# A down projection in seven block products for eight, with two of the weights' block sums made by accumulating transfers

## The chip, the cores and the metric

The kernel runs on one core of a Trainium2 chip. The metric is the device time of one execution in microseconds. A core has a matrix engine (TensorE, PE in the profile; its weight loads are the row PEld), a vector engine (VectorE, DVE), an activation engine (ScalarE, ACT), a general engine (GpSimd, POOL) and SyncE (SP), which here issues the DMA transfers. Each engine works through its own queue in order, and the engines wait for one another on semaphores.

## The reference

Two layers of a bidirectional encoder on one sequence of 512 positions with 1024 channels, all in float32. The first half of a layer (a Fourier group beside windowed attention, then an output projection) is not touched by the change. The second half is this:

```python
h = rmsnorm(x, norm2[l])                                   # 512 x 1024
up = dwconv_centred(h @ w_up[l], conv_w[l], conv_b[l])     # 512 x 5632, three taps along the positions
gate, val = up[..., :D_FF], up[..., D_FF:]                 # D_FF = 2816
x = x + (jax.nn.silu(gate) * val) @ w_down[l]              # w_down is 2816 x 1024
```

## The kernel before, in words

Activations lie transposed: 128 channels on the partitions, 512 positions along the free axis. So `x` is 8 tiles `x[m]` of 128x512, and the hidden width of 2816 is 22 tiles of 128.

Every large product is made in three passes. An operand is split into a rounded high half and the remainder, its low half: ScalarE writes the high half, VectorE subtracts it for the low one (`split` for activations, `wsplit` for weights, lines 90 and 93). `mm3` (lines 120 to 122) then multiplies high by high, low by high and high by low into one PSUM accumulation. The split weights live in the tags `whi` and `wlo`, with 5 slots of 512 columns each; raw weights come into `wraw`, 3 slots of 1024 columns, loaded on SP.

The feed-forward part runs over `HALVES`, two runs of 11 hidden tiles. For each hidden tile `fi` the gate tile and the value tile (`z` = 0 and 1) are made: 8 input tiles x 3 matmuls of 512 columns, then VectorE multiplies by the norm's scale (`u`, out of PSUM), ScalarE applies the middle tap and the bias, and VectorE adds the two outer taps (two `stt`, line 96). SiLU on ScalarE, one product of gate and value (on VectorE in layer 0, on POOL in layer 1) and a split into two halves give the tile `gu[k]`, stored in pieces of the tags `slab`, `pT` and `m4`. Temporary tiles of 512 columns come from the tag `tF`, with 6 slots.

After a run's 11 tiles come its 8 output tiles. For each `m`, the weights of 11 hidden tiles are loaded and split, 33 matmuls of 512 columns go into one PSUM bank, and VectorE adds the bank to `x[m]`. The banks are taken in turn from `FFN_BANKS`, six of them. At the end of layer 1 each `x[m]` is stored as soon as it is final, the last one in two halves of 256 positions. At the end of layer 0 each final `x[m]` is also scaled and split for the next layer (`norm_tile`).

In layer 0 a generator, `presplit`, prepares the weights of layer 1's first half in between: for each of 44 keys (16 `qkv`, 8 `u`, 4 `f`, 16 `o`) it loads the raw weights (two keys in one transfer, into `m4`), folds the `u` and `f` ones with two VectorE sums, splits the result into `tA` and stores both halves to DRAM, to be fetched in layer 1. `next(ahead)` does one key: before, once in three weight tiles of the up projection and twice for each output tile.

The program's order on each engine isn't the order of the source: a scheduler places the instructions at build time, along the dependencies and the free slots.

Of the kernel before, what the change touches and what calls it, by code (L numbers as in the profile page):

```python
# [16 lines left out]
P = 128  # L17
D = 1024
S = 512
# [15 lines left out]
HALVES = [(0, 11), (11, 11)]  # L35


def encoder_kernel(tc, t):
# [29 lines left out]
    def f(x):  # L68
# [5 lines left out]
             "tA": (512, 6), "tF": (512, 6), "sq": (512, 2)}  # L74
# [74 lines left out]
    def presplit(l):  # L149

        late = []

        def keep(key, src):
            n = src.shape[-1]
            two = [temp(n, "tA", F32R) for _ in range(2)]
            split(two[0], two[1], src)
            kept[key] = [dp.tile([P, n], F32, tag=f"{key}{s}", name=nm("kept")) for s in range(2)]
            store()
            late.append(lambda: [nc.sync.dma_start(o, f(z)) for o, z in zip(kept[key], two)])

        def store():
            while late:
                late.pop()()

        def cols(src, n, step):
            def load():
                raw = temp(1024, "m4")
                nc.sync.dma_start(raw[:, :n], src)
                return [raw[:, c:c + step] for c in range(0, n, step)]
            return load  # L170

        def prepare(kind, raw):
            if kind == "u":
                return fold_wu(raw)
            return fold_wf(raw) if kind == "f" else raw

        jobs = []
        for grp in (1, 0):
            for kk in range(KT // 2):
                jobs.append((cols(t["w_qkv"][l, grp, kk], 768, 384), [f"qkv{grp}{2 * kk + i}" for i in range(2)]))  # L180
        for kk in range(KT // 2):
            jobs.append((lambda kk=kk: load_wu(l, kk, temp(1024, "m4")), [f"u{2 * kk + i}" for i in range(2)]))
        for j in range(NF):
            jobs.append((lambda j=j: [load_wf(l, j, temp(1024, "m4"))], [f"f{j}"]))
        for half in range(2):
            for mp in range(KT // 2):
                jobs.append((cols(t["w_o"][l, half, :, mp * 1024:(mp + 1) * 1024], 1024, 512),
                             [f"o{half}{2 * mp + i}" for i in range(2)]))
        got = jobs[0][0]()
        for n, (_, keys) in enumerate(jobs):  # L190
            for i, key in enumerate(keys):
                keep(key, prepare(key[0], got[i]))
                if i == len(keys) - 1 and n + 1 < len(jobs):
                    got = jobs[n + 1][0]()
                yield
        store()
        while True:
            yield
# [179 lines left out]
    for l in range(L):  # L378
# [326 lines left out]
        for f0, nf in HALVES:  # L705
            gu = []
            for fi in range(f0, f0 + nf):
                ys_ = []
                n = fi - f0
                for z in range(2):  # L710
# [18 lines left out]
                if n < 4:  # L729
                    a = pair("slab")  # L730
                elif n < 8:
                    if n % 2 == 0:
                        two = temp(2048, "pT", F32R).rearrange("p (n s q) -> p n s q", n=2, s=2)
                    a = two[:, n % 2]
                else:
                    a = pair("m4")
                split(a[:, 0, :], a[:, 1, :], ys_[0])
                gu.append(a)
            nxt = []
            for m in range(KT):  # L740
                next(ahead)
                next(ahead)
                w = []
                for c in range(0, nf, 8):
                    n = min(8, nf - c)
                    w += wchunks(t["w_down"][l, m, :, (f0 + c) * P:(f0 + c + n) * P], n * P)
                end = l == L - 1 and f0 + nf == FT
                nh = 2 if end and m == KT - 1 else 1
                for h in range(nh):
                    q0, q1 = h * S // nh, (h + 1) * S // nh  # L750
                    nps[0] += 1
                    o = psum(FFN_BANKS[nps[0] % len(FFN_BANKS)])[:, q0:q1]
# [4 lines left out]
                    if end:  # L757
                        nc.sync.dma_start(t["out"][m, :, q0:q1], x[m][:, q0:q1])
                if l < L - 1 and f0 + nf == FT:
                    nxt.append(norm_tile(m, g1[:, l + 1, :], acc))  # L760
            xg = nxt
# [88 lines left out]
```

## Time and profile before

| | |
|---|---|
| runs shown, median (lowest to highest) | 1057.82 us (1056.07 to 1059.76) |
| the profiled execution | 1056.14 us, of which 1054.3 us are the span of the trace |
| PE busy | 1038.2 us (98%) |
| DVE busy | 726.8 us (69%) |
| ACT busy | 507.9 us (48%) |
| POOL busy | 90.8 us (9%) |
| granted clock of PE | 0.999 |
| transfers | 140.03 MB, nearly all issued by SP |

The busy time of an engine is the union of its instructions' durations. A matmul's shown duration is longer than the distance to the next one's start, since matmuls are pipelined; what a row of them costs is that distance. The same holds in a smaller measure for VectorE. Names such as `wlo<-wraw,whi` give the output and inputs of an instruction by the program's tags, `ps` is PSUM, and a name after `<-` in brackets is what ended the engine's idle time before that instruction.

### The profile page before, as it was taken

The numbers are of one execution on the slowest core, as the hardware profiler recorded it, in microseconds if no ns is written. First come the engines' busy times: TensorE is split into PE (matmuls) and PEld (weight loads), VectorE is DVE, ScalarE is ACT, GpSimd is POOL, SyncE is SP. The second block draws the span as 40 slices with busy tenths as digits, with TensorE's granted clock in tenths as the row PEclk, the third lists the DMA queues.
The fourth block names the chain that finished last, engine by engine and source line by source line (L and its number), as shares of the span: only waits on it lengthen the run. The fifth ranks groups of instructions, "written<-read, shape, count | busy, mean of one in ns | idle before, by whom it ended". The sixth has DMA issues, their size and how long they took to land.

```text
span 1054.3 us, 14425 instructions
## 1 busy us (share of the span) xinstructions
PE 1038.2 (98%) x5107; PEld 873.2 (83%) x5107; DVE 726.8 (69%) x1384; ACT 507.9 (48%) x939; POOL 90.8 (9%) x164
## 2 busy tenths in 40 slices
PE   8998999999999999999999999999999999999998
PEld 8986778888888888888899887888888888888887
DVE  8878768697767777777519775478877336878632
ACT  5339755455444445455423785246554224454421
POOL 0004410000000000000000152001101000101100
PEclk9999999999999999999999999999999999999999
DMA  7232152332269833239856313333332333332241
GB/s 273 83 115 87 58 193 81 100 100 96 78 226 353 324 100 101 89 114 322 280 181 221 113 62 99 122 100 94 101 101 74 96 115 100 98 101 82 82 150 48
DMA packets 60475, 140.03 MB, mean 133 GB/s; under 512 B 6642, under 2 KB 22258, under 8 KB 60404
## 3 DMA queue, kind: packets, MB, share of 16 engines
q1 hardware_dynamic: 60404, 139.12, 40.5%
q8 instruction: 40, 0.66, 0.3%
q14 instruction: 31, 0.25, 0.1%
HBM read 116.02 MB, written 23.07 MB: 132 GB/s over the span
## 4 chain that ended last, share of the span: by engine, by line
PE 93%; DVE 2%; DMA 2%; ACT 1%; issue 1%; POOL 0%; SPq 0%; ACTq 0%; DVEq 0%; POOLq 0%
PE ps L122 28%; PE ps L120 28%; PE ps L121 28%; PE ps L118 3%; PE ps L548 2%; PE ps L541 2%; PE ps L529 1%; DMA wraw<-in_w_qkv_dram 1%; PE ps L234 1%; PE ps L227 1%; ACT tA L90 0%; DMA x<-in_xT_dram 0%; DVE tA L533 0%; ACT act L90 0%; PE ps L500 0%
## 5 line engine op out<-in xcount | busy, mean ns | idle before, releaser
L90 ACT ACTIVATE whi<-wraw 128x512 fp32r<-128x512 f32 (+1 forms) x296 | 182.0, 616 | 290.8 <-PE ps L122 278.4
L120 PE MATMUL ps<-act,whi 128*128 128x512 f32 x768 | 298.9, 390 | 0.0
L121 PE MATMUL ps<-act,wlo 128*128 128x512 f32 x768 | 298.3, 389 | 0.0
L122 PE MATMUL ps<-act,whi 128*128 128x512 f32 x768 | 298.2, 389 | 0.0
L93 DVE TENSOR_TENSOR wlo<-wraw,whi 128x512 fp32r<-128x512 f32 (+1 forms) x304 | 219.7, 726 | 103.4 <-ACT whi L90 102.0
L122 PEld LDWEIGHTS ps<-act,whi 128*128 128x128 f32 x768 | 144.2, 188 | 30.1
L120 PEld LDWEIGHTS ps<-act,whi 128*128 128x128 f32 x768 | 144.2, 188 | 29.7
L121 PEld LDWEIGHTS ps<-act,wlo 128*128 128x128 f32 x768 | 144.2, 188 | 29.7
L96 DVE SCALAR_TENSOR_TENSOR tF<-tF,pb,tF 128x511 f32<-128x511 f32 x176 | 133.5, 763 | 11.1 <-ACT tF L90 8.7
L93 DVE TENSOR_TENSOR tF<-ps,rb 128x512 f32<-128x512 f32 x104 | 71.2, 689 | 77.9 <-PE ps L122 64.7
L120 PE MATMUL ps<-slab,whi 128*128 128x512 f32 (+2 forms) x212 | 82.2, 388 | 0.0
L122 PE MATMUL ps<-slab,whi 128*128 128x512 f32 (+2 forms) x212 | 79.9, 380 | 0.4 <-DVE slab L93 0.3
L121 PE MATMUL ps<-slab,wlo 128*128 128x512 f32 (+2 forms) x212 | 80.0, 378 | 0.0
L90 ACT ACTIVATE tF<-tF,pb 128x512 f32<-128x512 f32 x88 | 71.7, 816 | 11.3 <-DVE tF L93 4.6
L93 DVE TENSOR_TENSOR x<-x,ps 128x512 f32<-128x512 f32 (+1 forms) x49 | 32.9, 674 | 36.5 <-PE ps L122 36.3
L93 POOL TENSOR_TENSOR tF<-tF,tF 128x512 f32<-128x512 f32 x22 | 30.2, 1371 | 256.1 <-DVE tF L96 224.1
L120 PE MATMUL ps<-pT,whi 128*128 128x512 f32 (+1 forms) x132 | 50.5, 383 | 0.0
L121 PE MATMUL ps<-pT,wlo 128*128 128x512 f32 (+1 forms) x132 | 50.5, 383 | 0.0
L122 PE MATMUL ps<-pT,whi 128*128 128x512 f32 (+1 forms) x132 | 50.5, 383 | 0.0
L538 POOL TENSOR_SCALAR tA<-tA,den 128x256 f32<-128x256 f32 (+1 forms) x64 | 37.4, 590 | 145.1 <-DVE den L537 144.6
L533 DVE CUSTOM_DVE_ANT_0 tA<-ps,pb,nsink 128x256 f32<-128x256 f32 (+1 forms) x64 | 37.8, 603 | 14.5 <-PE ps L529 9.7
L122 PEld LDWEIGHTS ps<-slab,whi 128*128 128x128 f32 x212 | 39.7, 188 | 8.3 <-DVE slab L93 0.9
(178 smaller groups left out, 1485.0 us busy)
## 6 DMA issues: line engine op xcount, KB each, us to landing
wraw<-in_w_up_dram SPq DMA_DIRECT2D x88, 512.0 KB, 3.5
wraw<-in_w_down_dram SPq DMA_DIRECT2D x32, 512.0 KB, 3.7
kept<-tA SPq DMA_DIRECT2D x56, 256.0 KB, 5.7
whi<-kept SPq DMA_DIRECT2D x28, 256.0 KB, 3.0
wlo<-kept SPq DMA_DIRECT2D x28, 256.0 KB, 3.0
kept<-tA SPq DMA_DIRECT2D x32, 192.0 KB, 4.4
wraw<-in_w_down_dram SPq DMA_DIRECT2D x32, 192.0 KB, 2.4
wraw<-in_w_o_dram SPq DMA_DIRECT2D x8, 512.0 KB, 3.7
```

The lines of the kernel that those rows point to most:

```text
L90: return nc.scalar.activation(out, in_, func, **kw)
L93: return (eng or nc.vector).tensor_tensor(out, a, b, op=op)
L96: return nc.vector.scalar_tensor_tensor(out=out, in0=a, scalar=s, in1=b, op0=op0, op1=op1)
L118: nc.tensor.matmul(out, a[0], b[0], start=start, stop=stop, **kw)
L120: nc.tensor.matmul(out, a[0], b[0], start=start, stop=False, **kw)
L121: nc.tensor.matmul(out, a[1], b[0], start=False, stop=False, **kw)
L122: nc.tensor.matmul(out, a[0], b[1], start=False, stop=stop, **kw)
L227: nc.tensor.matmul(pt[:, 2 * b:2 * b + 2], acc[:, b * P:(b + 1) * P], ones2, start=True, stop=True)
L533: nc.vector.tensor_tensor_reduce(out=pr[:, :n], in0=sc[:, :n], in1=mask[:, m0:m0 + n], scale=qs_scale[p][:, i, e:e + 1], scalar=nsink[:, l ...
L538: nc.gpsimd.tensor_scalar(pr[:, :n], pr[:, :n], den[:, i:i + 1], 1.0, op0=ALU.mult, op1=ALU.mult)
L541: tr = nc.tensor.transpose(pp[:, j * P:(j + 1) * P], pr[:, j * P:(j + 1) * P], ident)
L548: pv = nc.tensor.matmul(py[64 * e:64 * e + 64, i0 * P:(i1 + 1) * P], vp[:, j, 64 * g:64 * g + 64], pT[:, half, e, b0:b0 + 2 * (i1 - i0) + ...
```

## The change

The hidden tiles are now taken in three groups of 8, 8 and 6 (`GROUPS`), and in each group the down projection of two output tiles is treated as a product of 2x2 blocks. Of the weights, a block is one output tile by half of the group's hidden tiles (`kp` = 4, 4 or 3 of them): `a11, a12` belong to the even output tile, `a21, a22` to the odd one. Of the activations, a block is half of the group's hidden tiles by half of the positions (256 columns). Seven products of such blocks give the four output blocks, where the plain way takes eight.

Four sums of activation blocks are needed (`T1` to `T4`), made once a group by VectorE from each pair of hidden tiles (`seven_gu`), and then split: 7 halves of 256 columns for each pair, high and low, in the pieces that `pieces` hands out. For this the hidden tiles are made in the order 0, kp, 1, kp+1 and so on, so that a pair is complete after two tiles.

Four sums of weight blocks are needed for each pair of output tiles (a block row, four in a group; `seven_w`). `a21 + a22` is made by loading `a21` into `s1` on SP and then letting a transfer issued by POOL add `a22` onto it from DRAM. `s2 = a11 - s1` and `s3 = a11 - a21` are made by VectorE. When `s2` has been split for its own product, another transfer from POOL adds `a12` onto it. Each of the seven weight blocks is split by `wsplit`, which reads 512 or 384 columns.

The products go into three running sums, X, Y and Z. X and Y are the two halves of one PSUM tile, Z is half of another. After each product VectorE adds the sum as it then stands to a quarter of the two `x` tiles (128x256): X after products 0, 2, 4 and 6, Y after 1 and 5, Z after 3.

`presplit` now loads one key at a time, into a tag of its own (`praw`, 2 slots), and `next(ahead)` stands three times in four weight tiles of the up projection and once for each block row. The product of gate and value is on VectorE in both layers. The norm tiles at the end of layer 0 come two at a time, after a block row.

```diff
-HALVES = [(0, 11), (11, 11)]
+GROUPS = [(0, 8), (8, 8), (16, 6)]
...
-             "tA": (512, 6), "tF": (512, 6), "sq": (512, 2)}
+             "tA": (512, 6), "tF": (512, 6), "sq": (512, 2), "praw": (512, 2)}
...
+    LANDED = {3: (0, 0), 4: (1, 1), 5: (0, 1), 6: (1, 0)}
+    def pieces(kp):
+        for tag, n in (("slab", 2), ("pT", 5), ("m4", 2)):
+            for _ in range(TEMPS[tag][1]):
+                whole = temp(512 * n, tag, F32R)
+                yield from [whole[:, i * 512:(i + 1) * 512] for i in range(n)]
+
+    def seven_gu(b1, b2, room):
+        t13, t24 = temp(512, "tF"), temp(512, "tF")
+        lo, hi = slice(0, 256), slice(256, 512)
+        tt(t13[:, lo], b1[:, hi], b1[:, lo], ALU.subtract)
+        tt(t13[:, hi], b2[:, hi], b1[:, hi], ALU.subtract)
+        tt(t24[:, lo], t13[:, lo], b2[:, hi], ALU.subtract)
+        tt(t24[:, hi], t24[:, lo], b2[:, lo], ALU.add)
+        g = {}
+        one = next(room)
+        g["B11"] = [one[:, lo], one[:, hi]]
+        split(*g["B11"], b1[:, lo])
+        for src, keys in ((b2, ("B21", "B22")), (t13, ("T1", "T3")), (t24, ("T2", "T4"))):
+            two = [next(room), next(room)]
+            split(*two, src)
+            for key, cols in zip(keys, (lo, hi)):
+                g[key] = [z[:, cols] for z in two]
+        return g
+
+    def seven_w(l, m, f0, kp):
+        n = kp * P
+        a, b = [wload(t["w_down"][l, m + i, :, f0 * P:f0 * P + 2 * n], 2 * n) for i in range(2)]
+        s1 = temp(n, "tF")
+        nc.sync.dma_start(s1, t["w_down"][l, m + 1, :, f0 * P:f0 * P + n])
+        nc.gpsimd.dma_start(s1, t["w_down"][l, m + 1, :, f0 * P + n:f0 * P + 2 * n], accum_op=ALU.add)
+        a11, a12, a21, a22 = a[:, :n], a[:, n:], b[:, :n], b[:, n:]
+        yield "X", wsplit(a11), "B11", 0, 0
+        yield "Y", wsplit(s1), "T1", 1, 1
+        s2 = temp(n, "tF")
+        tt(s2, a11, s1, ALU.subtract)
+        yield "X", wsplit(s2), "T2", 0, 1
+        yield "Z", wsplit(a12), "B21", 0, 0
+        s3 = temp(n, "tF")
+        tt(s3, a11, a21, ALU.subtract)
+        yield "X", wsplit(s3), "T3", 1, 1
+        nc.gpsimd.dma_start(s2, t["w_down"][l, m, :, f0 * P + n:f0 * P + 2 * n], accum_op=ALU.add)
+        yield "Y", wsplit(s2), "B22", 0, 1
+        yield "X", wsplit(a22), "T4", 1, 0
...
-        for f0, nf in HALVES:
+        for f0, nf in GROUPS:
+            kp = nf // 2
+            room = pieces(kp)
             gu = []
-            for fi in range(f0, f0 + nf):
+            for n in range(nf):
+                fi = f0 + n // 2 + kp * (n % 2)
...
-                    if (2 * n + z) % 3 == 2:
+                    if (2 * n + z) % 4 < 3:
                         next(ahead)
                 act(ys_[0], ys_[0], AF.Silu)
-                tt(ys_[0], ys_[0], ys_[1], ALU.mult, nc.gpsimd if l else nc.vector)
...
+                tt(ys_[0], ys_[0], ys_[1], ALU.mult)
+                if n % 2 == 0:
+                    upper = ys_[0]
                 else:
-                    a = pair("m4")
-                split(a[:, 0, :], a[:, 1, :], ys_[0])
-                gu.append(a)
+                    gu.append(seven_gu(upper, ys_[0], room))
             nxt = []
-            for m in range(KT):
-                next(ahead)
+            for mp in range(KT // 2):
                 next(ahead)
...
-                    for k in range(nf):
-                        mm3(o, [z[:, (k % 4) * P:(k % 4 + 1) * P] for z in w[k // 4]],
-                            [gu[k][:, s, q0:q1] for s in range(2)], k == 0, k == nf - 1)
-                    tt(x[m][:, q0:q1], x[m][:, q0:q1], o, ALU.add)
...
+                xy, zz = [psum(FFN_BANKS[(nps[0] + i) % len(FFN_BANKS)]) for i in (1, 2)]
+                nps[0] += 2
+                bank = dict(X=xy[:, :256], Y=xy[:, 256:], Z=zz[:, :256])
+                for i, (b, w, g, r, c) in enumerate(seven_w(l, 2 * mp, f0, kp)):
+                    m, q0 = 2 * mp + r, 256 * c
+                    for k in range(kp):
+                        mm3(bank[b], [z[:, k * P:(k + 1) * P] for z in w], gu[k][g], k == 0 and i in (0, 3), k == kp - 1,
+                            skip_group_check=True)
+                    tt(x[m][:, q0:q0 + 256], x[m][:, q0:q0 + 256], bank[b], ALU.add)
+                    if l == L - 1 and f0 + nf == FT and i in LANDED:
+                        m, q0 = 2 * mp + LANDED[i][0], 256 * LANDED[i][1]
+                        nc.sync.dma_start(t["out"][m, :, q0:q0 + 256], x[m][:, q0:q0 + 256])
                 if l < L - 1 and f0 + nf == FT:
-                    nxt.append(norm_tile(m, g1[:, l + 1, :], acc))
+                    nxt += [norm_tile(m, g1[:, l + 1, :], acc) for m in (2 * mp, 2 * mp + 1)]
```

The rewritten `presplit` (one key a load) is left out of this cut.

More of the change, by code (lines that the diff above doesn't have):

```diff
@@ L163, in store, with load @@
                 late.pop()()
[L165 to L175, printed above, removed]
+        def load(src):
+            raw = temp(512, "praw")[:, :src.shape[-1]]
+            nc.sync.dma_start(raw, src)
+            return raw
@@ L177, in presplit @@
         jobs = []
         for grp in (1, 0):
[L179 to L182, printed above, removed]
+            for k in range(KT):
+                c = (k % 2) * 384
+                jobs.append((f"qkv{grp}{k}", lambda g=grp, k=k, c=c: load(t["w_qkv"][l, g, k // 2, :, c:c + 384])))
@@ L183, in presplit @@
+        for k in range(KT):
+            jobs.append((f"u{k}", lambda k=k: load(t["w_in"][l, k * P:(k + 1) * P, 0:FW])))
         for j in range(NF):
-            jobs.append((lambda j=j: [load_wf(l, j, temp(1024, "m4"))], [f"f{j}"]))
+            jobs.append((f"f{j}", lambda j=j: load_wf(l, j, temp(512, "praw"))))
         for half in range(2):
-            for mp in range(KT // 2):
-                jobs.append((cols(t["w_o"][l, half, :, mp * 1024:(mp + 1) * 1024], 1024, 512),
-                             [f"o{half}{2 * mp + i}" for i in range(2)]))
@@ L189, in presplit @@
[L189 to L195, printed above, removed]
+            for m in range(KT):
+                jobs.append((f"o{half}{m}", lambda h=half, m=m: load(t["w_o"][l, h, :, m * 512:(m + 1) * 512])))
+        got = jobs[0][1]()
+        for n, (key, _) in enumerate(jobs):
+            raw = got
+            if n + 1 < len(jobs):
+                got = jobs[n + 1][1]()
+            keep(key, fold_wu(raw) if key[0] == "u" else fold_wf(raw) if key[0] == "f" else raw)
+            yield
@@ L704, in encoder_kernel @@
         ahead = presplit(l + 1) if l < L - 1 else iter(lambda: 0, 1)
-        for f0, nf in HALVES:
+        for f0, nf in GROUPS:
+            kp = nf // 2
+            room = pieces(kp)
             gu = []
-            for fi in range(f0, f0 + nf):
+            for n in range(nf):
+                fi = f0 + n // 2 + kp * (n % 2)
                 ys_ = []
-                n = fi - f0
                 for z in range(2):
@@ L724, in encoder_kernel @@
                     ys_.append(y)
-                    if (2 * n + z) % 3 == 2:
+                    if (2 * n + z) % 4 < 3:
                         next(ahead)
                 act(ys_[0], ys_[0], AF.Silu)
-                tt(ys_[0], ys_[0], ys_[1], ALU.mult, nc.gpsimd if l else nc.vector)
[L729 to L734, printed above, removed]
-                else:
-                    a = pair("m4")
@@ L737, in encoder_kernel @@
-                split(a[:, 0, :], a[:, 1, :], ys_[0])
-                gu.append(a)
+                tt(ys_[0], ys_[0], ys_[1], ALU.mult)
+                if n % 2 == 0:
+                    upper = ys_[0]
+                else:
+                    gu.append(seven_gu(upper, ys_[0], room))
             nxt = []
-            for m in range(KT):
+            for mp in range(KT // 2):
                 next(ahead)
-                next(ahead)
[L743 to L752, printed above, removed]
-                    for k in range(nf):
-                        mm3(o, [z[:, (k % 4) * P:(k % 4 + 1) * P] for z in w[k // 4]],
-                            [gu[k][:, s, q0:q1] for s in range(2)], k == 0, k == nf - 1)
-                    tt(x[m][:, q0:q1], x[m][:, q0:q1], o, ALU.add)
-                    if end:
-                        nc.sync.dma_start(t["out"][m, :, q0:q1], x[m][:, q0:q1])
@@ L759, in encoder_kernel @@
                 if l < L - 1 and f0 + nf == FT:
-                    nxt.append(norm_tile(m, g1[:, l + 1, :], acc))
-            xg = nxt
+                    nxt += [norm_tile(m, g1[:, l + 1, :], acc) for m in (2 * mp, 2 * mp + 1)]
+        xg = nxt
     for cm in reversed(ctxs):
```

## The prediction

> **What bounds the kernel now.** I read the page's busy table and its chain first, then the windows of the feed-forward stages, then the timeline of single instructions.
>
> ```profile
> span 1054.3 us, 14425 instructions
> PE 1038.2 (98%) x5107; PEld 873.2 (83%) x5107; DVE 726.8 (69%) x1384; ACT 507.9 (48%) x939; POOL 90.8 (9%) x164
> PE 93%; DVE 2%; DMA 2%; ACT 1%; issue 1%; POOL 0%; SPq 0%; ACTq 0%; DVEq 0%; POOLq 0%
> ```
>
> The chain that ended last is 93% matmuls. In the windows (columns: stretch, length, busy time and count of PE, PEld, DVE, ACT, POOL, clock, DMA share, GB/s) PE is never idle in the feed-forward part of either layer:
>
> ```profile
> 195.00:295.00 100.00, 100.00 (x447) 82.92 (x446) 78.39 (x120) 53.31 (x81) 0.00 (x0) 1.00 0.30 94
> 300.00:358.00 58.00, 58.00 (x257) 48.03 (x256) 41.31 (x89) 25.22 (x46) 0.00 (x0) 1.00 0.98 348
> 720.00:815.00 95.00, 95.00 (x421) 78.67 (x420) 80.29 (x107) 51.22 (x76) 14.29 (x11) 1.00 0.29 92
> 820.00:875.00 55.00, 55.00 (x244) 45.56 (x243) 20.11 (x31) 13.92 (x23) 0.00 (x0) 1.00 0.33 104
> ...
> 200.00:210.00 10.00, 10.00 (x46) 8.26 (x45) 10.00 (x17) 8.22 (x12) 0.00 (x0) 1.00 0.29 85
> 210.00:220.00 10.00, 10.00 (x46) 8.29 (x45) 10.00 (x18) 5.74 (x9) 0.00 (x0) 1.00 0.30 87
> ```
>
> So PE time removed here is time gained, as long as nobody keeps PE waiting. The last two rows matter for that: VectorE was saturated for 20 us in a backlog and PE lost nothing.
>
> **Term 1, the matmuls.** Their price is the pitch from start to start, not the shown duration. The end of the down projection has both widths, because its last output tile is already cut into two halves of 256:
>
> ```profile
> 1035.73 0.39 PE L121 MATMUL ps<-slab,wlo 128*128 128x512 f32 x1
> ...
> 1042.76 0.39 PE L122 MATMUL ps<-m,whi 128*128 128x512 f32 x1
> 1042.98 0.28 PE L120 MATMUL ps<-slab,whi 128*128 128x256 f32 x1
> ...
> 1049.46 0.28 PE L120 MATMUL ps<-pT,whi 128*128 128x256 f32 x1
> ```
>
> 31 steps in 7.03 us are 0.2267 us for 512 columns; 54 steps in 6.48 us are 0.120 us for 256, each with a weight load of its own, so the doubled number of loads is in this price. Before: 8 tiles x 22 x 3 x 2 layers = 1056 matmuls of 512, 33 of them cut into 66 halves: 1023 x 0.2267 + 66 x 0.120 = 239.8 us. After: 7 products x 3 x (4+4+3 tile pairs) x 4 block rows x 2 layers = 1848 at 0.120, 221.8 us. Gain 18.1 us. All other terms are losses against it.
>
> **Term 2, VectorE.** Its price is a pitch too:
>
> ```profile
> 246.01 0.69 DVE L93 TENSOR_TENSOR tF<-ps,rb 128x512 f32<-128x512 f32 x1 [0.76 <-PE ps L122]
> 246.61 0.68 DVE L93 TENSOR_TENSOR pT<-tF,pT 128x512 fp32r<-128x512 f32 x1
> 247.22 0.68 DVE L93 TENSOR_TENSOR wlo<-wraw,whi 128x512 fp32r<-128x512 f32 x1
> 247.82 1.53 DVE L96 SCALAR_TENSOR_TENSOR tF<-tF,pb,tF 128x511 f32<-128x511 f32 x2
> 249.39 0.69 DVE L93 TENSOR_TENSOR wlo<-wraw,whi 128x512 fp32r<-128x512 f32 x1
> ...
> 312.34 0.55 DVE L93 TENSOR_TENSOR tA<-m,tA 128x384 fp32r<-128x384 f32 x1
> 312.81 0.69 DVE L93 TENSOR_TENSOR wlo<-wraw,whi 128x512 fp32r<-128x512 f32 x1
> ...
> 320.01 0.75 DVE L93 TENSOR_TENSOR tA<-m 128x255 f32<-128x255 f32 x2
> 320.68 0.69 DVE L93 TENSOR_TENSOR wlo<-wraw,whi 128x512 fp32r<-128x512 f32 x1
> ```
>
> 0.605 us for 512 columns, 0.47 for 384, 0.335 for 256, 1.57 for the pair of convolution steps. Up, per tile of the hidden width: 4 low halves of weights, 2 evacuations, 2 convolution pairs, 1 gating product, 4x0.605 + 1.2 + 3.14 + 0.6 = 7.4 us; before also one split (0.6), with the few prepared keys 8.3 of PE's 48 x 0.2267 = 10.88 (measured: 78.39 of 100). After, the split gives way per pair to four 256 sums, one 256 low half and three of 512, 5x0.335 + 3x0.605 = 3.5, or 1.75 a tile: 9.1 in layer 1. In layer 0, 33 instead of 14 prepared keys now fall into up (16 at 0.47, 8 folded `u` and 4 folded `f` at 2x0.335 + 0.605 and a small one, 1.4, 5 at 0.6: 27 us over 22 tiles), 10.4 of 10.88; the second group, with the folded keys, is over by about 0.4 x 8 tiles = 3 us.
>
> Down, per block row of four pairs: 7 low halves, 2 sums, 7 additions of 256, 9x0.605 + 7x0.335 = 7.8, plus 0.6 for a key in layer 0, against 84 x 0.120 = 10.08. With three pairs: 9x0.47 + 2.35 = 6.6 against 7.56. The last group of layer 0 also has two norm tiles (0.75 + 0.6 each, 2.7) and a key, 9.9: over by 2.4 x 4 = 9.6 us. Ends for the two overruns: 0 and 13. I take 2, near the lower end, because the saturated windows cost nothing and norms and keys can run on into the next projection, where VectorE has room.
>
> ScalarE: up 4x0.63 + 2x0.82 + 0.63 + 1.1 per tile, below 7 of 10.88 with the keys; down 4.4 to 7 of 7.56 or 10.08; nothing on the path.
>
> ```profile
> L90 ACT ACTIVATE whi<-wraw 128x512 fp32r<-128x512 f32 x256 | 161.2, 631 | 252.6 <-PE ps L122 247.7 <-DMA wraw<-in_w_down_dram 2.0 <-PE ps L118 1.3
> L90 ACT ACTIVATE tF<-tF,pb 128x512 f32<-128x512 f32 x88 | 71.7, 816 | 11.3 <-DVE tF L93 4.6 <-DVE tF L96 0.6
> ...
> L93 DVE TENSOR_TENSOR wlo<-wraw,whi 128x512 fp32r<-128x512 f32 x53 | 47.1, 889 | 17.5 <-ACT whi L90 17.1
> ...
> L93 DVE TENSOR_TENSOR wlo<-wraw,whi 128x512 fp32r<-128x512 f32 x108 | 74.4, 689 | 14.1 <-ACT whi L90 13.3
> ```
>
> The gating product of layer 1 goes from POOL to VectorE, 22 x 0.6 = 13 us more there. The last two rows are the weights' low halves in layer 1 after 878 us (889 ns) and in layer 0 (689 ns); the slow ones stand beside POOL's products (POOL 14.29 us busy in the 720 window), so about 0.2 us on each of some hundred comes back. Even; and POOL is free for the transfers.
>
> **Term 3, the hand-offs.** X and Y are halves of one PSUM tile, a running sum that is read after each product. If a read and a product in the same tile may not overlap, product 1 waits for the addition after product 0, 2 for 1, 4 for 2, 5 for 4 and 6 for 5. One hand-off from rows:
>
> ```profile
> 1046.82 0.28 PE L122 MATMUL ps<-m,whi 128*128 128x256 f32 x1
> 1047.14 0.42 DVE L93 TENSOR_TENSOR x<-x,ps 128x256 f32<-128x256 f32 x1 [3.27 <-PE ps L122]
> ...
> 117.32 1.89 DVE L93 TENSOR_TENSOR slab<-tF,slab 128x512 fp32r<-128x512 f32 x3
> 118.06 0.19 PEld L122 LDWEIGHTS ps<-slab,whi 128*128 128x128 f32 x1 [0.31 <-DVE slab L93]
> ```
>
> PE could go on at 1046.94; the addition ends at 1047.56; PE follows a VectorE result after 0.05 us (117.32 + 0.69 to 118.06): 0.67 us if nothing fills it. A filler is 9 or 12 matmuls, 1.08 or 1.44 us, so one is enough. Product 3, in Z, fills one of five; the others need the next block row, which has other banks (three pairs of six), but only five slots for split weights, so its first products are prepared late. Ends: 0, and 4 x 24 x 0.67 = 64 us. I take one open hand-off for two block rows, 12 x 0.67 = 8 us, near the lower end since PE's order before was interleaved where a tile was late.
>
> **Term 4, from up to down, six times.** The last activations need an evacuation, ACT's scaling, the convolution, the product, the two T1/T3 sums and a split: 0.6 + 0.82 + 1.57 + 0.6 + 0.67 + 0.63 + 0.69 = 5.6 us. PE has meanwhile product 0 whole (B11 comes from the earlier tile) and all but the last pair of 1 to 3: 12 + 27 matmuls, 4.7 us, or 9 + 18, 3.2 us; with the next row's product 0, 6.1 or 4.3. Between 2 x 1.3 and 2 x (0.9 + 0.9 + 2.4): I take 3.
>
> **Term 5, transfers.**
>
> ```profile
> wraw<-in_w_up_dram SPq DMA_DIRECT2D x88, 512.0 KB, 3.5
> kept<-tA SPq DMA_DIRECT2D x56, 256.0 KB, 5.7
> whi<-kept SPq DMA_DIRECT2D x28, 256.0 KB, 3.0
> m<-in_w_in_dram SPq DMA_DIRECT2D x4, 512.0 KB, 6.6
> ```
>
> SP issues three loads a block row for four, `w_down` moves seven blocks for four (104 GB/s of the 820 window to some 180), and of the keys' loads and stores only 12 of 44 stay in down: its share was 0.98 with PE full, so it eases; in up it rises from 0.30 to about 0.55 and the `w_up` loads queue behind keys on SP, three buffers ahead. Zero. POOL issues two accumulating transfers a row, none in the trace. The second starts when S2 is split and is used by product 5. Landing is bounded by 3.0 and 6.6 us, then 1.3 for a split; PE has products 2 to 4 in between (4.3 or 3.2 us) and up to four prepared ones ahead (another 5.8 or 4.3). With the lead: 0 for either. Without it: at 3.0, 8 x 1.1 = 9 us; at 6.6, 16 x 3.6 + 8 x 4.7 = 95 us. I take 0; POOL blocks nobody but its other transfer. [...]
>
> **Sum.** -18.1 + 2 + 8 + 3 + 0 = -5 us. The profiled execution took 1056.1 (span 1054.3 and 1.8 around it), 1.7 below the median of the three runs; from the two I forecast 1051 to 1053, and write 1052.
>
> **The rivals.**
> - *Everything hidden.* The hand-offs are all filled and VectorE's overruns vanish in the backlog: 1057.8 - 18 = 1040. For it: the saturated windows. Against: no stage had a chain of reads as tight as this.
> - *It comes out even.* One open hand-off per block row (16 us), 4 for overruns and transitions, +2: 1055 to 1061.
> - *The shared bank becomes the bound.* Place: products 1, 2, 4, 5, 6 of each block row. It decides from 1.1 open hand-offs a row on, with 2 a row 32 us, net +19, 1077; with 4, 1109. For it: five weight slots, and VectorE at 77 to 96%, where an addition queues behind a 0.6 us instruction. Against: three pairs of banks. [...]
> - *The accumulating transfer is late.* Half of the 95 us: 1057.8 - 5 + 48 = 1100. For it: nothing in the trace bounds it well. Against: plain loads of that size land in 3.0 us.
> - *Seven for eight isn't cheaper*, because a weight load of 188 ns must stand behind 256 columns: excluded by the 0.120 pitch.
>
> **How the numbers follow.** Forecast case (1045 to 1054) 0.30; all hidden 0.22; even 0.18; shared bank 0.19; late transfers 0.11. Less than 0.3%, 3.2 us, can't be told from no change here. Faster 0.52, same 0.18, slower 0.30. The range runs from 1039 (all hidden) to 1077 (two open hand-offs a row), which leaves out the worse halves of the last two. The likeliest case's own range is 1045 to 1054.
>
> **What would show it.** 1848 matmuls of 256 at a pitch of 0.120; PE under 100% only in the down windows, with gaps of 0.3 to 0.7 us released by the x additions (hand-offs), or by split weights behind a POOL transfer (late transfers); VectorE near 96% in layer 0's up. The forecast is wrong if PE in a down window is below 90% or at 100% throughout.

## The result, and the profile after

The changed kernel takes 1212.39 us (median of 4 runs, 1207.49 to 1217.4) against 1056.98 us on the same chip: 1.1467 times as long, 95% interval 1.1446 to 1.1488. The forecast was 1052 us, with 1077 as the upper end. The page of the changed kernel (busy times, then tenths in 40 slices, then the shares of the chain that ended last):

```profile
span 1205.6 us, 16704 instructions
PE 1062.4 (88%) x5866; PEld 919.9 (76%) x5866; DVE 876.3 (73%) x1793; ACT 557.4 (46%) x1055; POOL 105.3 (9%) x190
PE   8999989990899967999589999999969998699967
PEclk9999999995799988999899999999979999899979
PE 35%; DMA 7%; DVE 5%; issue 3%; ACT 1%; POOL 0%; SPq 0%; POOLq 0%; ACTq 0%; DVEq 0%
```

The span grew by 151.3 us. PE's idle time went from 16.1 (1054.3 - 1038.2) to 143.2 us (1205.6 - 1062.4): 127 of the 151. The other 24 are in PE's busy time, though the matmuls are 18 us less work. By the trace's clock records PE was busy for 55 us at half clock, which at a pitch of 0.213 for 0.120 us is 24 us of lost time; the remaining 18 are, by estimate, what 68 more interruptions leave as ends of a shown matmul beyond its pitch (0.28 - 0.12 to 0.58 - 0.21 us each, 11 to 25 us). The row of PE has a hole at each of six places, where a group's up projection (up) ends and its down projection (down) begins; these places are called seams below. The row of the clock is below 9 at or right after the same places.

How the two layers took it is read from two windows, each from the last attention product of a layer to the first of the next, or to the end (columns as in the prediction: stretch, length, PE, PEld, DVE, ACT, POOL, clock, DMA share, GB/s). Before:

```profile
145.00:610.30 465.30, 462.58 (x2241) 393.19 (x2237) 330.08 (x599) 225.78 (x384) 9.65 (x22) 1.00 0.51 168
661.40:1051.10 389.70, 389.66 (x1767) 324.05 (x1763) 246.74 (x344) 159.72 (x245) 32.18 (x24) 1.00 0.31 98
```

After:

```profile
145.30:701.60 556.30, 476.68 (x2635) 416.85 (x2631) 408.98 (x795) 251.15 (x445) 32.95 (x46) 0.94 0.54 159
752.50:1202.40 449.90, 399.84 (x2130) 347.37 (x2126) 318.68 (x558) 184.81 (x303) 22.83 (x26) 0.94 0.38 104
```

So 91 us were lost in layer 0, which has the next layer's presplit beside it, and 60 in layer 1, which has none. In the windows of up PE stays full; the loss sits at the seams. One of them, layer 1's first, in windows of 10 us and then in the timeline of all engines (matmuls left out between the last before and the first after the gap):

```profile
860.00:870.00 10.00, 10.00 (x48) 8.32 (x47) 6.21 (x11) 3.20 (x5) 0.00 (x0) 1.00 0.11 44
870.00:880.00 10.00, 1.19 (x10) 0.98 (x9) 6.34 (x12) 2.60 (x4) 1.81 (x2) 0.76 0.36 78
880.00:890.00 10.00, 7.71 (x36) 7.21 (x36) 5.96 (x11) 3.18 (x6) 0.86 (x1) 0.56 0.63 132
```

```profile
869.80 0.69 DVE L93 TENSOR_TENSOR tF<-ps,rb 128x512 f32<-128x512 f32 x1 [2.27 <-PE ps L122]
...
870.91 0.28 PE L122 MATMUL ps<-m,whi 128*128 128x256 f32 x1
...
873.13 1.49 DVE L93 TENSOR_TENSOR tF<-tF,tF 128x512 f32<-128x512 f32 x3
873.18 2.77 SPq L407 DMA_DIRECT2D tF<-in_w_down_dram  x2
...
876.33 0.94 POOL L408 DMA_DIRECT2D tF<-in_w_down_dram  x1 [75.49 <-ACT m L90]
...
880.75 0.69 DVE L93 TENSOR_TENSOR tF<-wraw,tF 128x512 f32<-128x512 f32 x1 [3.80 <-DMA tF<-in_w_down_dram]
880.81 1.36 ACT L90 ACTIVATE whi<-tF 128x512 fp32r<-128x512 f32 x2 [4.59 <-DMA tF<-in_w_down_dram]
881.36 0.69 DVE L93 TENSOR_TENSOR tF<-wraw,wraw 128x512 f32<-128x512 f32 x1
881.49 0.58 PE L120 MATMUL ps<-slab,whi 128*128 128x256 f32 x1 [10.30 <-DVE tF L93]
```

The sum `s1` is the weight of product 1, and its slot comes from `tF`, whose six slots hold up's evacuations and convolution results. SP can issue its load only at 873.18, when the last outer tap is done, after 14.4 us of waiting for the slot; POOL's accumulating transfer goes at 876.33 and its data are there at 880.75. PE had done product 0 by 871.19 and then stood for 10.30 us: 2.0 until the load was issued, 3.2 until the accumulating transfer was, 4.4 until its data were there, and 0.7 for the split. The kernel as a whole, in the waits and the transfers (KB, median us from issue to landing):

```profile
ACT whi L90 <- DMA tF<-in_w_down_dram: 96.7, 26, 7.2
POOL tF L408 <- DMA tF<-in_w_down_dram: 84.2, 18, 7.7
PE ps L120 <- DVE tF L93: 39.9, 5, 10.3
PE ps L120 <- ACT whi L90: 38.4, 14, 9.6
```

```profile
tF<-in_w_down_dram POOLq DMA_DIRECT2D x32, 256.0 KB, 4.3
tF<-in_w_down_dram SPq DMA_DIRECT2D x16, 256.0 KB, 5.3
```

The load's 5.3 us are a median over both layers; in the seam shown it landed after 2.6 us, and the rest of that gap is the wait for the slot and the accumulating transfer.

After the gap, the same matmuls go at half the pace for a while (PE alone in the timeline):

```profile
883.72 0.41 PE L122 MATMUL ps<-pT,whi 128*128 128x256 f32 x1
883.93 0.41 PE L120 MATMUL ps<-pT,whi 128*128 128x256 f32 x1
...
889.07 0.28 PE L121 MATMUL ps<-m,wlo 128*128 128x256 f32 x1
889.19 0.28 PE L122 MATMUL ps<-m,whi 128*128 128x256 f32 x1
```

The steps are 0.213 us up to 888.6 and 0.120 from then on, as the granted clock of 0.56 in the window from 880 to 890 says.

### The profile page after: what moved, and what is told of

The parts are those of the page before. It is cut to its first block, busy times and chain, and to the rows that moved or that the text cites. A ratio compares the mean times of both kernels' runs of the same rounds, so it can differ in the third digit from the quotient of the medians.

```text
span 1205.6 us, 16704 instructions
## 1 busy us (share of the span) xinstructions
PE 1062.4 (88%) x5866; PEld 919.9 (76%) x5866; DVE 876.3 (73%) x1793; ACT 557.4 (46%) x1055; POOL 105.3 (9%) x190
## 4 chain that ended last, share of the span: by engine, by line
PE 35%; DMA 7%; DVE 5%; issue 3%; ACT 1%; POOL 0%; SPq 0%; POOLq 0%; ACTq 0%; DVEq 0%
PE ps L120 11%; PE ps L122 11%; PE ps L121 11%; DMA tF<-in_w_down_dram 5%; DMA wraw<-in_w_down_dram 2%; DVE wlo L93 2%; PE ps L596 1%; PE ps L589 1%; DVE tF L93 1%; ACT whi L90 1%; DVE x L93 1%; DMA whi<-kept 1%; PE ps L577 1%; DVE tF L96 0%; PE ps L227 0%
## 5 line engine op out<-in xcount | busy, mean ns | idle before, releaser
L93 DVE TENSOR_TENSOR wlo<-wraw,whi 128x512 fp32r<-128x512 f32 (+1 forms) x280 | 185.6, 668 | 34.4 <-ACT whi L90 33.1
L120 PE MATMUL ps<-slab,whi 128*128 128x256 f32 (+2 forms) x272 | 92.4, 344 | 89.1 <-DVE tF L93 39.7
L90 ACT ACTIVATE whi<-tF 128x512 fp32r<-128x512 f32 (+1 forms) x96 | 56.9, 592 | 163.6 <-DMA tF<-in_w_down_dram 96.7
L93 DVE TENSOR_TENSOR x<-x,ps 128x256 f32<-128x256 f32 (+1 forms) x184 | 80.8, 441 | 57.5 <-PE ps L122 56.1
L121 PE MATMUL ps<-slab,wlo 128*128 128x256 f32 (+2 forms) x272 | 89.5, 329 | 11.1 <-DVE wlo L93 11.1
L122 PE MATMUL ps<-slab,whi 128*128 128x256 f32 (+2 forms) x272 | 87.1, 323 | 0.4 <-DVE slab L93 0.3
L120 PE MATMUL ps<-pT,whi 128*128 128x256 f32 x264 | 79.9, 303 | 6.6 <-ACT pT L90 6.6
L93 DVE TENSOR_TENSOR wlo<-tF,whi 128x512 fp32r<-128x512 f32 (+1 forms) x96 | 61.3, 644 | 29.5 <-ACT whi L90 28.8
L121 PE MATMUL ps<-pT,wlo 128*128 128x256 f32 x264 | 79.7, 302 | 0.0
L121 PEld LDWEIGHTS ps<-slab,wlo 128*128 128x128 f32 x272 | 55.3, 203 | 17.4 <-DVE wlo L93 15.2
L408 POOL DMA_DIRECT2D tF<-in_w_down_dram x24 | 21.1, 880 | 539.5 <-ACT m L90 284.7
```

The source lines that it names most:

```text
L90: return nc.scalar.activation(out, in_, func, **kw)
L93: return (eng or nc.vector).tensor_tensor(out, a, b, op=op)
L120: nc.tensor.matmul(out, a[0], b[0], start=start, stop=False, **kw)
L121: nc.tensor.matmul(out, a[1], b[0], start=False, stop=False, **kw)
L122: nc.tensor.matmul(out, a[0], b[1], start=False, stop=stop, **kw)
L408: nc.gpsimd.dma_start(s1, t["w_down"][l, m + 1, :, f0 * P + n:f0 * P + 2 * n], accum_op=ALU.add)
```

## The experiments

All were compared with the kernel before on their own chip (1056 to 1058 us). Where two layer times stand, they are the lengths of the windows above, 465 and 390 us before, 556 and 450 after.

### What the sums of the weights cost, and where they lie

**e1_own**: the weights' sums get slots from another tag.

```diff
-        s1 = temp(n, "tF")     # s2, s3 alike
+        s1 = temp(n, "tA")
```

> s1, s2 and s3 come out of the tag tA (6 slots, nearly free in the feed-forward part, quite free in layer 1) instead of tF; nothing else. Theory 1 (the s1 transfer starts late because s1's slot is one of the six tF slots that the last tiles of up hold; PE then waits about 10 us and its clock is halved for some 13 us more): s1 lands before up ends, the five gaps of about 10 us at the ends of up shrink to below 4 us, the halved clock goes, and the time falls from 1212 to about 1120 to 1150. Rival (the accumulating transfers' own latency is the cost, wherever they start): the gaps stay above 8 us and the time stays within 1190 to 1215.

1145.4 us, ratio 1.0839 (1.0798 to 1.088); layers 516 and 426. So 67 us were a matter of slots. The theory had the seams' gaps below 4 us and the half clock gone: PE's longest gap at each seam fell only to 2.7 to 5.5 us, and the time at half clock from 121 to 87 us. In layer 0 this is not the slot of `s1` alone, though: `presplit` takes its halves from `tA` too, and the sums now hold it back. The rows of the stores of its keys (instructions in the window 145 to 300, first and last start) of the changed kernel and of e1_own:

```profile
L159 SPq DMA_DIRECT2D kept<-tA x79: 319/327/642, 145.3 to 286.6; - x79
```

```profile
L159 SPq DMA_DIRECT2D kept<-tA x25: 319/424/593, 146.3 to 295.8; - x25
```

In the changed kernel the generator raced through the keys by 287 us, ahead of the first group's own work, whose gap was 30 us instead of 10. The gain in layer 1, 24 us, has nothing to do with presplit.

**e2_dve**: all four sums on VectorE, no accumulating transfers, the slots still in `tF`.

```diff
-        nc.sync.dma_start(s1, ...a21...)
-        nc.gpsimd.dma_start(s1, ...a22..., accum_op=ALU.add)
+        tt(s1, a21, a22, ALU.add)
...
-        nc.gpsimd.dma_start(s2, ...a12..., accum_op=ALU.add)
+        tt(s2, s2, a12, ALU.add)
```

> All four weight sums by VectorE (two more 512-column sums per block row, 1.2 us of about 10), no accumulating transfer and no extra loads; the slots stay in tF. Theory 1: the slot still comes free late, but a sum takes 0.7 us where load and transfer take 7.5, so the gaps fall to 3 to 4 us: 1110 to 1140, about the same as with slots of their own. Rival (latency of the transfers): the same gain at the ends of up and also all waits within a block row gone: below 1100. Rival (VectorE bound): VectorE's share in the down windows goes from 65 to 80% and above and PE stays below 90% there: above 1150.

1155.97 us, ratio 1.0939 (1.0877 to 1.1001); layers 532 and 422. In layer 1 it does what e1_own does, and a little more. The time is that of the rival with VectorE as the bound, and its signs are there too: in layer 1's down windows VectorE is busy for 84 to 89% (61 to 64% in the changed kernel) and PE for 75 to 77%. The next run has the same work for VectorE, and only the slots differ; it is 35 us shorter (29 in layer 0, 6 in layer 1), so the amount of that work alone doesn't set the time.

**f_dve**: both together, sums on VectorE and slots from `tA`.

> As the kernel with s1 to s3 in tA, but all four weight sums by VectorE and no accumulating transfer. If the transfers still hold up products once s1 has its own slots: 1115 to 1135. If VectorE's 1.2 us more in each block row cost as much: 1140 to 1155.

1121.08 us, ratio 1.0607 (1.0576 to 1.0638); layers 503 and 416. The accumulating transfers cost 24 us even with slots of their own.

**h_w**: no sums of weights at all; the products take plain blocks in their place. This kernel, and h_wa and h_ws below, which leave out sums too, compute something else and are run for their times alone.

```diff
-        s1 = temp(n, "tF")                                        # and both transfers
-        s2 = temp(n, "tF"); tt(s2, a11, s1, ALU.subtract)         # s3 alike
+        s1, s2, s3 = a21, a11, a11
```

> The changed kernel with the four sums of the down weights' blocks left out: the seven products take plain blocks (a21, a11, a11, a11) for s1, s2, s3, s4, so there are neither accumulating transfers nor slots for the sums, and VectorE has 48 operations fewer in the down; the activations' sums stay. Theory (the sums of the weights, wherever they are made, are what is left between the version with all sums on VectorE, 1121 us, and the eight products with the same groups, 1065 us): 1080 to 1098 us, because the queue of VectorE at each end of up is 2 us shorter, and no gap there over 3 us. Rival (what is left is the chain of the activations' sums and the gating, with the halved clock after it): 1108 to 1122 us.

1114.51 us, ratio 1.055 (1.0522 to 1.0579): the rival's number. The layers tell why: 404 in layer 1, 12 below f_dve as the theory has it, but 511 in layer 0, 8 above it: without sums in `tA` the presplit races again (79 stores by 291 us), and the first group has gaps of 2.5, 4.3 and 9.3 us. What is left in layer 1, 14 us, isn't the weights' sums.

**h_wa**: as h_w, and the activations' sums are left out too (T1 to T4 are split from the gated tiles).

```diff
-        t13, t24 = temp(512, "tF"), temp(512, "tF")
-        tt(t13[:, lo], ...)                                       # four sums
+        t13, t24 = b2, b1
```

> As the kernel without the weights' sums, and the four sums of the activations are left out too: the factors T1 to T4 are split straight from the two gated tiles. Seven products with nothing before them but the gating and the splitting. Theory (matmuls of 256 themselves run at full pace): 1045 to 1075 us, with the seven products' 18 us of saved matmul time in sight against the 1065 us of the eight products. Rival (matmuls of 256, or their seven banks' additions, cost by themselves): 1085 us or more.

1106.69 us, ratio 1.0485 (1.0456 to 1.0515); layers 500 and 404. A miss of the theory, and layer 1 doesn't move against h_w at all: the activations' sums cost nothing there. The rival's condition is met, but not its reason, as g1 below shows with the same matmuls.

### The seam between up and down

**e4_pace**: presplit's keys held behind ScalarE's scaling of the tile beside which they stand.

```diff
-                        next(ahead)
+                        with tc.issue_after(shown.ins):
+                            next(ahead)
```

> The keys of presplit are held behind the scaling of the weight tile at which they stand in the source (an ordering edge on ScalarE); nothing else. Theory (in layer 0 all 44 keys run ahead into the first group's up and fill VectorE and SP's queue, so the first down starts 30 us late instead of 10): the first gap falls to about 10 us, the time to 1175 to 1190. Rival (the keys are not what delays it): the time stays at 1205 to 1215.

1201.17 us, ratio 1.1366 (1.1326 to 1.1407). The first seam's gaps went from 30 to 17 us, the second's from 10 to 17 and the third's from 10 to 12: the keys were only moved. Layer 0 gained 9 us, layer 1 none (450), and the time lies between theory and rival.

**f_yz**: e1_own with Y in Z's PSUM tile, so that X's reads and Y's products don't share one.

```diff
-                bank = dict(X=xy[:, :256], Y=xy[:, 256:], Z=zz[:, :256])
+                bank = dict(X=xy[:, :256], Y=zz[:, 256:], Z=zz[:, :256])
...
-  mm3(bank[b], ..., k == 0 and i in (0, 3), ...)
+  mm3(bank[b], ..., k == 0 and i in (0, 1), ...)
```

> As the kernel with s1 to s3 in tA, but Y lies in Z's bank instead of X's, so that no two products in a row write one bank. Theory (a product waits for the read of its bank by the addition before it): waits of PE for the x additions, 12 us in 19 waits in the changed kernel, nearly go, 1130 to 1140. Rival (the waits are only moved, since the split weights come no faster): 1143 to 1150.

1146.43 us, ratio 1.0847 (1.0804 to 1.0889), against 1145.4 of e1_own: no change. PE's waits for the `x` additions, which the theory had nearly gone, came to 32.7 us in 21 places, after 20.5 in 20 in e1_own. The shared bank isn't what bounds the down there.

**f_stag**: e1_own with the next group's first hidden tile made before the down.

```diff
+            if f0 + nf < FT:
+                g0, gn = GROUPS[GROUPS.index((f0, nf)) + 1]
+                early = up_tile(g0, gn // 2, 0)
             nxt = []
```

`up_tile` is the code that made one hidden tile before, now a function; the next group takes the early tile as its first. That part is left out of the cut.

> As the kernel with s1 to s3 in tA, and the first hidden tile of the next group (48 matmuls, 10.9 us) stands in the source ahead of a group's down, so that PE has work while the last activations go through their chain; possible at four of six ends. Theory (what is left of the gap is the chain of the last activations, 5.6 us by rows): the four gaps vanish, clock and all, 1095 to 1115. Rival (weight slots and wraw go to the early tile, and the down's first weights come late instead): gaps of the same size one place later, 1130 to 1160.

1138.81 us, ratio 1.0775 (1.0703 to 1.0846): 7 us, where 30 and more were expected, so the rival's number. The longest gap at the four covered seams fell from between 3.7 and 5.1 us to between 1.9 and 2.1, and the two without cover kept 5.4 and 3.2; but PE's waits for split weights rose from 18.7 us in 14 places to 26.4 in 22. Cover for PE helps little while the weights come late. Why the seam of e1_own is long at all is seen on VectorE alone, at layer 1's second seam:

```profile
977.73 0.74 DVE L96 SCALAR_TENSOR_TENSOR tF<-tF,pb,tF 128x511 f32<-128x511 f32 x1
980.91 0.69 DVE L93 TENSOR_TENSOR tA<-wraw,wraw 128x512 f32<-128x512 f32 x1 [2.44 <-DMA wraw<-in_w_down_dram]
981.52 0.68 DVE L93 TENSOR_TENSOR wlo<-tA,whi 128x512 fp32r<-128x512 f32 x1
982.12 0.74 DVE L96 SCALAR_TENSOR_TENSOR tF<-tF,pb,tF 128x511 f32<-128x511 f32 x1
```

Between the two outer taps of the last hidden tile stands the sum of a weight block that hasn't landed. VectorE waits 2.44 us for it, with the tap, the gating product, the activations' sums and their splits queued behind, and PE waits for those.

**h_ws**: h_w with the same early tile.

> As the kernel without the weights' sums, with the next group's first hidden tile put ahead of the down, so that TensorE has 10.9 us of work while the last activations' sums and splits are made (at the last group of a layer there is none, so two of the six ends of up keep their chain). Theory (the activations' chain at the end of each group is what the version without weights' sums still has): 15 to 25 us below that version. Rival (the chain is short, and the loss lies within the down's rows): within 8 us of it.

1097.24 us, ratio 1.0385 (1.0367 to 1.0402), 17 us below h_w; layers 501 and 394. Without weights' transfers and sums to wait for, the cover is worth what the theory said.

**g1**: f_dve, f_yz and f_stag in one, with the full arithmetic.

> All of the change's arithmetic: sums of the weights on VectorE in a tag of their own, Y's sums in Z's bank, and the next group's first hidden tile ahead of the down. Theory (in the version with all sums on VectorE, two weights' sums stand ahead of the activations' last sums in VectorE's queue, 3.5 us of idle TensorE and some 6 us of halved clock at each end of up; four of six ends get cover): 1080 to 1102 us. Rival (each part adds only what it brought alone, 7 us): 1112 to 1120 us. Below 1057 us it would beat the kernel before, which neither expects.

1077.42 us, ratio 1.019 (1.0164 to 1.0217), 44 us below f_dve, far more than the parts brought alone. Windows of the layers:

```profile
147.10:633.60 486.50, 465.77 (x2636) 409.72 (x2632) 411.93 (x820) 249.35 (x445) 9.50 (x22) 0.99 0.51 163
684.40:1074.90 390.50, 384.56 (x2130) 336.38 (x2126) 326.01 (x582) 186.13 (x303) 2.02 (x2) 0.99 0.31 98
```

Layer 1 is back at 390.5 for 389.7 us, with PE 5.1 us less busy and 5.9 us idle, most of it in one gap of 4.4 us at the last group, which has no next tile to cover it. Layer 0 is still 21 us over.

### What isn't the seven products

**e5_plain**: the three groups, the new presplit and VectorE's gating, with eight products of 512 columns.

> The eight block products as before (matmuls of 512, no sums, no accumulating transfers, one PSUM bank an output tile), but with the three groups of 8, 8 and 6, the new presplit with praw, and the gating product on VectorE. If the groups and presplit carry part of the loss: above 1075. If the seven products alone carry it: 1052 to 1065, with PE at 100% in the feed-forward windows.

1065.48 us, ratio 1.0082 (1.0053 to 1.0112); layers 473 and 390. So some 9 of the 155 us come from what was changed around the products, nearly all in layer 0.

**m1**: layer 0 as before the change in everything, layer 1 as in g1.

```diff
+        if l == 0:
             ...                       # HALVES, eight products, the presplit of before
+        else:
+            ...                       # GROUPS, seven products, as g1
```

> Layer 0 as in the kernel before (halves of eleven tiles, eight products, the presplit of before), layer 1 with seven products as in the staggered version with all sums on VectorE (1077 us). Theory (seven products lose in layer 0 because VectorE is over 95% busy there beside the presplit, and break even in layer 1, 390.5 us for 389.7 us): 1055 to 1062 us. Rival (the surplus of layer 0 belongs to what both layers share, and layer 1 alone shows it too once layer 0 is quick): 1064 us or more.

1057.8 us (11 runs), ratio 1.0002 (0.9992 to 1.0011); layers 465 and 390. What g1 still lost belongs to layer 0, which has the presplit beside it, and seven products in layer 1 are even within the runs' noise.

### The halved clock

**f_fill**: e1_own with 24 dummy matmuls of 512 after the first product of each group; **m2** and **g2**: m1 and g1 with 18 in the last groups.

```diff
+  fill = psum("tp")
+  for _ in range(24):
+      nc.tensor.matmul(fill, h2[0][:, 0, :P], h2[0][:, 0, :], start=True, stop=True)
```

> As the kernel with s1 to s3 in tA (1145 us, 87 us of its span at half clock), and after product 0 of each group's first block row 24 matmuls of 512 columns into a PSUM tile that nobody reads: 5.4 us of PE time without use, six times. Theory (a gap of 4 to 6 us on PE costs its own length and about the same again, since the clock is halved behind it): PE has no gap over 3 us at the ends of up, the time at half clock falls below 40 us, and the kernel gets faster although it does more, to 1105 to 1125. Rival (the halved clock hides behind waits): no change or up to 30 us slower, 1140 to 1175.

> As the version with seven products in layer 1 alone, with 18 dummy matmuls of 512 (18 x 0.2267 = 4.1 us) on TensorE inside the gap of the last group, right before the last pair's first matmul, into a bank nobody reads. Theory (after a gap of 4.4 us the clock is halved for 6.8 us, which costs 3.4 us of matmul work, and the gap itself stays): 2.0 to 4.5 us below the version without them, so 1052 to 1058 us. Rival (the clock's loss is not paid at the end, the dummies only take time): the same within 1 us, or up to 4 us more.

> The staggered version with all sums on VectorE (1077 us) in both layers, with the same 18 dummy matmuls in the gap of each layer's last group, right before the last pair's first matmul. Theory (gaps of 4.3 and 4.4 us, each followed by 6.8 us of halved clock): 4 to 8 us less, 1069 to 1073 us, and no half clock at these two places. Rival: within 2 us of 1077 us.

1157.78 (ratio 1.0954, 1.0919 to 1.0989), 1062.01 (1.0044, 1.003 to 1.0059) and 1083.81 us (1.0248, 1.0229 to 1.0266): 12, 4 and 6 us more than without. m2 and g2 didn't test what they were meant to, and f_fill did so at two of six seams. The dummies depend on nothing late, and the scheduler issued them early: in m2 and g2 in a layer's first group, where PE had work. m2's row has them at 791.7 us, and the gap at 1020:

```profile
L864 PE MATMUL ps<-act x18: 389/389/397, 791.7 to 795.5; 128*128 128x512 f32 x18
```

m2 shows only that 18 matmuls of 512 on a full PE cost their 4.1 us. In f_fill all 72 dummies of a layer went to its first seam and none to the other two. There they did fill the gap: in layer 1 they are 16.3 us of matmuls and the layer is 3 us longer than in e1_own (429 for 426), with 8.7 us less idle time of PE and 8.7 us less of its busy time at half clock (13.9 for 22.6), which is 3.8 us of lost time. The filler was too long for its gap, and the time is the rival's.

**m3** and **g3**: m1 and g1 with 19 dummies held behind the last matmul ahead of the gap.

```diff
+  with tc.issue_after(done.ins):
+      for _ in range(19):
+          nc.tensor.matmul(fill, ...)
```

> As m1 (seven products in layer 1 alone), with 19 dummy matmuls of 512 (19 x 0.2267 = 4.3 us) in the gap of layer 1's last group, now held behind the last matmul that goes ahead of the gap. Theory (a gap of 4.4 us is followed by 6.8 us of halved clock, which costs 3.4 us of matmul work; the gap's own time stays): no half clock at that place, 2 to 4 us below m1, so 1053.5 to 1056 us. Rival (the useful matmuls that now lie between the dummies and the end, or the dummies' own time, take it back): within 1 us of m1.

> As the staggered version with all sums on VectorE in both layers (1077 us), with the same 19 dummy matmuls in the gaps of both layers' last groups, held behind the last matmul ahead of each gap. Theory: two places at 3.4 us of lost matmul work, 4 to 7 us below it, 1070 to 1073.5 us. Rival: within 2 us of 1077 us.

1056.46 us, ratio 0.9995 (0.9986 to 1.0003), and 1077.19 us, 1.019 (1.0175 to 1.0206): 1.3 us below m1, between theory and rival and no more than the runs can tell apart, and even with g1, the rival's number. The windows at the gap say what they did. m1:

```profile
1016.00:1021.00 5.00, 0.57 (x6) 0.37 (x4) 4.93 (x10) 1.15 (x2) 0.00 (x0) 0.87 0.00 0
1021.00:1026.50 5.50, 5.14 (x21) 4.73 (x22) 4.19 (x10) 2.20 (x4) 0.00 (x0) 0.50 0.26 74
```

m3:

```profile
1016.00:1021.00 5.00, 4.66 (x28) 3.87 (x26) 4.97 (x11) 1.56 (x3) 0.00 (x0) 1.00 0.00 0
1021.00:1026.50 5.50, 4.47 (x21) 4.12 (x22) 4.08 (x9) 2.20 (x4) 0.00 (x0) 0.69 0.25 73
```

The gap is full, yet the clock still falls for part of the next 5.5 us, after a remaining wait of 1.03 us for a split activation; and the layer took 390.1 for 390.2 us, since the matmuls after the gap still had to wait for the activations: both kernels did 21 in that window. The price in the theory was also too high: 6.8 us at half clock were put at 3.4 us, but PE was busy for only 5.2 of them in m1, 2.3 us of lost time. In g3 the clock stays full at layer 1's gap, and layer 1 took 389.2 for 390.5 us in g1, less than the runs of a kernel differ. That the half clock costs time is seen in the pitches (0.213 for 0.120 us); that filling a gap wins time on the whole was not shown.

## Why the prediction was wrong, by its own steps

**Term 1 (matmuls, -18.1) held.** Full-clock matmuls of 256 columns kept the pitch of 0.120 (889.07 to 889.19 in the rows above). In g1's layer 1, PE is busy for 384.6 us with some 2 us of clock loss in it (4.4 us busy at half clock), so 7 below before's 389.7 without that loss; half of 18.1 was expected per layer.

**Term 5 (transfers, 0) is the step that failed**, at two of its sentences. "SP issues three loads a block row", with nothing in front of them: the load into `s1` needs a slot of `tF`, and those are up's until the seam, so product 1's weight wasn't prepared ahead but was the last thing to be started. And "POOL blocks nobody but its other transfer": PE, ScalarE and VectorE all queue behind what POOL's transfer delivers. The upper end of 95 us was priced for the second transfer, of product 5, alone; nothing was set down for the first one, whose chain of slot, load, accumulation and split shows as 9.4 to 10.3 us at the five seams after layer 0's first. The runs put 67 us on the slots (with presplit's share in it) and 24 on the transfers beyond that. The accumulating transfers of 256 KB landed after 4.3 us at the median. At 4.3 us the second transfer without lead would have been priced at 40 us (16 x 1.3 and 8 x 2.4, by the same cover), still without the seam.

**Term 4 (seams, 3 us, ends 2.6 to 8.4) was mis-sized.** It let the 5.6 us chain of the last activations run undisturbed and had PE cover it with products 1 to 3, whose weights weren't there. With the weights' sums on VectorE (f_dve) PE's longest gap is 3.0 to 4.1 us at each of the six seams, because three or more weight operations, 0.6 us each or waiting for a load, stand in VectorE's queue between the steps of that chain. That VectorE had room on average (70 to 80% busy) said nothing about the order in that queue.

**The clock was not priced.** Every term was reckoned at 0.120 or 0.2267 us a matmul. The clock fell during each of the five gaps of 9.4 to 10.3 us and stayed at half for 4.0 to 7.3 us after it, up to 3 us of lost time each, and other gaps did their part: 24 of the 155 us in all.

**Term 2 (VectorE, +2) was too small.** Groups, presplit and gating without the seven products cost some 9 us (e5_plain), and presplit didn't spread over 22 tiles as assumed but ran through in the first group: all 88 stores by 294 us in e5_plain, by 512 in the kernel before. Which of the three costs the 9 us, and whether by way of VectorE, no run separates.

**Term 3 (hand-offs, +8) came near in size, in part by luck**, and its rival, the shared bank, didn't come. PE waits for the `x` additions for 12.4 us in 19 places:

```profile
PE ps L120 <- DVE x L93: 12.4, 19, 1.5
```

The mean of 0.65 us is the 0.67 of the prediction. But in e1_own, with the same additions, they are 20.5 us, and in f_yz, where they have no shared bank as their cause, 32.7 us at the same time of the kernel: the bank doesn't set them, and what they cost by themselves no run shows.

**The late-transfer rival** (0.11, 1100 us) had the right mechanism, gaps behind a POOL transfer, at the wrong place: product 5 in each row for product 1 at each seam. The condition in the text, PE below 90% in a down window, is met by the window 870 to 880 with 1.19 of 10. Even with all of its 95 us the sum would have been 1148.

What stays open: layer 0's last 13 us in g1 over e5_plain (486.5 against 473), and how much of f_dve to g1 is Y's bank and how much the early tile; with e1_own as the base they brought 0 and 7, and together on f_dve 44.

## What to carry to other kernels

Before a step is called hidden, ask of its first instance in each stage which slot it writes to and who frees that slot: a buffer shared with the stage before turns prefetch into a chain of load, transfer and split at the seam. Fewer matmuls win only if the added operations find their place in the in-order queues: here even the best version of seven products (m1, m3, in one layer of the two) only broke even, and it had all sums off the transfers and a tile of other work at the seam. A gap on TensorE is to be priced with the slower matmuls after it (here 0.213 for 0.120 us a matmul, for 7.3 us after the gap of 10.3 us shown), and a filler is tested only when its place in the trace has been looked up.

## What the runs showed of the hardware

An accumulating transfer from DRAM of 256 KB lands after 4.3 us at the median, and takes POOL 0.88 us to issue:

```profile
L408 POOL DMA_DIRECT2D tF<-in_w_down_dram x24 | 21.1, 880 | 539.5 <-ACT m L90 284.7
```

With the gap of 10.3 us shown above, the clock was at 0.5 for 13.7 us, from 4 us after the gap's start; with 4.4 us (m1) for 6.8, from 3 us after its start. In m3, where the longest wait left at that place was 1.03 us, the clock still came to 0.69 over 5.5 us.

The clock records of the changed kernel's trace, from 150 us on, tell more than the length of a gap does. The clock in them is 1.0 or 0.5, and its 22 changes lie whole multiples of 3.41 us apart. At full clock, a step of that grid in which PE was busy for less than 45% was followed by half clock in 9 of 9 cases, one with 45 to 65% in 2 of 10, and one with more in none of 253. At half clock, full clock followed each of the 10 steps in which PE was busy for 95% or more, and 1 of the 25 others (one with 91%). In the kernel before, PE was busy for more than 65% of each of 263 such steps, and the clock was at 1.0 after each. So in this trace a few short waits close together could cost the clock as one long gap did: after waits of 1.20 and 1.12 us between 1185.62 and 1188.32 it was at 0.5 for 3.41 us, from 1189.19 on.
